# Attention scores as three fp32r matmuls instead of one fp32 matmul, masks added by VectorE

## The chip, the cores and the metric

The program runs on one core of one Trainium2 chip, as one launch. The metric is device time in microseconds (us), the median of several runs. TensorE (PE) multiplies, and its weight loads are a row of their own (PEld). VectorE (DVE), ScalarE (ACT) and GpSimd (POOL) do the elementwise work, and SyncE (SP) issues nearly all DMAs. Each engine takes its instructions in the order in which a scheduler wrote them down when the program was built.

## The reference

Two layers of a mixer with a gated feed-forward net, then retention, another feed-forward net, a short convolution and a mixture of eight experts. All is float32, 256 tokens, width 1024. The change lies in the mixer, which has three branches. Two of them are attentions and one is an mLSTM:

```python
# sparse attention, 8 heads of 64: the 64 best keys of an index score are kept
s = jnp.einsum('bqhd,bqkhd->bhqk', qb, k_sel) * (dh ** -0.5)
s = jnp.where(valid[:, None], s, -jnp.inf); p = jax.nn.softmax(s, axis=-1)
# differential attention, 4 heads x 2 parts of 64, causal
s = jnp.einsum('bqhcd,bshcd->bhcqs', qb, k) * (d ** -0.5)
s = jnp.where(causal, s, -jnp.inf);        p = jax.nn.softmax(s, axis=-1)
a = p[:, :, 0] - lam * p[:, :, 1]
# mLSTM, 4 heads of 128, chunks of 128: a causal mask on the decay matrix
dmat = jnp.where(causal, b_t - b_s + i_s, -jnp.inf)
```

## The kernel before

**Large matmuls.** A weight is loaded as float32 (`raw`, SP's queue, line 210), ScalarE rounds it to fp32r (`hi`, line 222) and VectorE takes the rest (`lo`, line 223). `mm3` (lines 228 to 231) then multiplies hi by hi, hi by lo and lo by hi into one PSUM tile. There are three buffers each of `hi` and `lo`. This work runs through the whole program.

**The mixer.** It runs once per layer, so twice. `ORDER` mixes the chunks of the wide projection with steps of three generators: `dsa` (sparse attention), `diff` (differential attention) and `mlstm`. A scheduler then sets the order on each engine, so that the matmuls of the projection stand between the steps of the attentions.

**Scores.** `qk_rows` normalises and rotates q and k, and `plain_T` (lines 297 to 306) transposes them on TensorE and copies them to SBUF as float32 (`sqT`, `skT`, `dqT`, `dkT`). A head has 64 elements, so its score matmul uses 64 of the 128 rows of the array, the upper or the lower half. Queries come in two tiles `t` of 128, tile 0 against 128 keys and tile 1 against 256. Per layer `dsa` has 8 groups (tile `t`, `q`) of two heads, and `diff` has 8 groups (tile, pair of heads `hp`, part `c`) of two. That is 64 score matmuls over both layers, half of them with 128 keys. After each one a bf16 matmul of the identity `idb` with the mask (`smask` line 607, `negm` line 673) adds 0 or -1e30 into the same PSUM tile. Then VectorE finds the row maximum (`nm`, lines 609 and 675), ScalarE takes the exponential (lines 612 and 678), and TensorE transposes the result (line 543) for the product with v.

**mLSTM.** For each of 4 heads two matmuls with 4 rows (`lf` by `selr`, lines 785 and 787) spread a decay, and after each a bf16 matmul adds `negmT` (lines 786 and 788). ScalarE's exponential (lines 790 and 791) follows.

Of the kernel before, what the change touches and what calls it, by code (L numbers as in the profile page):

```python
# [11 lines left out]
F32R = mybir.dt.float32r  # L12
BF16 = mybir.dt.bfloat16
# [102 lines left out]
class Net:  # L116
# [58 lines left out]

    def masks(self):
        nc, cp = self.nc, self.cp
        self.idb = cp.tile([P, P], BF16, name="idb")
        nc.vector.tensor_copy(self.idb, self.idt)
        self.negm = cp.tile([P, P], BF16, name="negm")  # L180
        nc.vector.tensor_scalar(self.negm, self.lo01, -1.0, BIG, op0=ALU.add, op1=ALU.mult)
        self.negmT = cp.tile([P, P], BF16, name="negmT")
        nc.vector.tensor_scalar(self.negmT, self.up01, -1.0, BIG, op0=ALU.add, op1=ALU.mult)
        self.cap = cp.tile([P, P], F32, name="cap")
        nc.vector.tensor_scalar(self.cap, self.lo01, -0.5, 2.0 * FILL, op0=ALU.add, op1=ALU.mult)
# [238 lines left out]
    def mixer(self, li):  # L424
        nc, tc, I, sp = self.nc, self.tc, self.I, self.sp
        X = self.X
        with ExitStack() as es:
# [5 lines left out]
            def z4(name, shape=(P, 2, 512), dt=F32):  # L433
                return zp_.tile(list(shape), dt, tag="z4", name=name)
# [92 lines left out]
                nc.scalar.activation((skr if c0 == 0 else sv)[:, t], ps, AF.Copy, scale=crs[:, t:t + 1])  # L527
            self.gemm(lambda k: (ch[:, k], cl[:, k]), 2, I["dsa_w_kv_up"][li], [(0, 512), (512, 512)], ev_kv)

            def qk_rows(src, which, dstT):  # L530
                rows = [w2("qkr") for _ in range(2)]
                for t in range(2):
                    normrope(src[:, t], which, rows[t], t)
                self.plain_T(lambda t: rows[t], 4, dstT)

            def pT_of(prow, npair, t):

# [15 lines left out]
            def dsa():  # L553

                smask, scs = [None, None], [None, None]
                for t in range(2):
# [15 lines left out]
                    dsl = slice(t * P, (t + 1) * P)  # L572
                    nc.vector.tensor_tensor(sc[:, dsl], sc[:, dsl], self.cap, op=ALU.min)
                    scs[t] = sc
                sqT, skT = z4("sqT", (P, 4, S)), z4("skT", (P, 4, S))
                qk_rows(zs, 0, sqT)
                yield
                qk_rows(skr, 1, skT)
                yield
                for t in range(2):  # L580
                    nk = P * (t + 1)
# [13 lines left out]
                for t in range(2):  # L595
# [3 lines left out]
                    for q in range(4):  # L599
                        heads = [(q // 2) * 4 + (q % 2) + 2 * j for j in range(2)]  # L600
                        b = slice((q % 2) * 64, (q % 2) * 64 + 64)
                        ps = self.mm_tile()
                        psv = ps.rearrange("p (j s) -> p j s", j=2)[:, :, :nk]
                        for j in range(2):
                            hp = heads[j] // 2
                            nc.tensor.matmul(psv[:, j], sqT[b, hp, t * P:(t + 1) * P], skT[b, hp, :nk], start=True, stop=False)
                            nc.tensor.matmul(psv[:, j], self.idb, smask[t][:, :nk], start=False, stop=True)
                        nm = tp.tile([P, 2], F32, tag="nm", name="nm")
                        nc.vector.tensor_reduce(nm, psv, AX.X, ALU.max, negate=True)
                        pr = w2("pr", (P, 2, 256))  # L610
                        for j in range(2):
                            nc.scalar.activation(pr[:, j, :nk], psv[:, j], AF.Exp, bias=nm[:, j:j + 1],
                                                 accum_out=den[:, heads[j]:heads[j] + 1])
                        pt = pT_of(pr, 2, t)
                        for j, h in enumerate(heads):
                            for s in range(t + 1):
                                nc.tensor.matmul(po[:, h * 64:(h + 1) * 64], pt[:, j, s], sv[:, s, h * 64:(h + 1) * 64],
                                                 start=s == 0, stop=s == t)
                        if q < 3:
                            yield  # L620
# [18 lines left out]
            def diff():  # L639
# [10 lines left out]

                go = tp.tile([P, 1], F32, tag="go", name="go", bufs=1)
                nc.vector.tensor_scalar(go, self.gcol("diff_out_norm_g", li), 1.0 - lam_init, None, op0=ALU.mult)
                dqT, dkT = z4("dqT", (P, 4, S)), z4("dkT", (P, 4, S))
                qk_rows(dq[0], 2, dqT)
                yield
                qk_rows(dk[0], 3, dkT)
                yield
                orow = z4("orow")
                for t in range(2):
                    nk = P * (t + 1)  # L660
                    po = self.mm_tile()
                    for hp in range(2):
# [3 lines left out]
                        for c in range(2):  # L666
# [1 line left out]
                            psv = ps.rearrange("p (j s) -> p j s", j=2)[:, :, :nk]  # L668
                            b = slice(c * 64, c * 64 + 64)
                            for j in range(2):  # L670
                                nc.tensor.matmul(psv[:, j], dqT[b, hp * 2 + j, t * P:(t + 1) * P], dkT[b, hp * 2 + j, :nk],
                                                 start=True, stop=False)
                                nc.tensor.matmul(psv[:, j, t * P:(t + 1) * P], self.idb, self.negm, start=False, stop=True)
                            nm = tp.tile([P, 2], F32, tag="nm", name="nm")
                            nc.vector.tensor_reduce(nm, psv, AX.X, ALU.max, negate=True)
                            pr = w2("dp", (P, 2, 256))
# [97 lines left out]
            def mlstm():  # L774
# [3 lines left out]
                for hp in range(2):  # L778
                    pn = [self.mm_tile() for _ in range(2)]
                    for j in range(2):  # L780
# [1 line left out]

                        pw = self.mm_tile()
                        sel = self.selr[:, h * P:(h + 1) * P]
                        nc.tensor.matmul(pw[:, 0:S], sel, lf[:, 0], start=True, stop=False)
                        nc.tensor.matmul(pw[:, 0:P], self.idb, self.negmT, start=False, stop=True)
                        nc.tensor.matmul(pw[:, S:S + P], sel, lf[:, 0, P:S], start=True, stop=False)
                        nc.tensor.matmul(pw[:, S:S + P], self.idb, self.negmT, start=False, stop=True)
                        wt = w2("wt")[:, 0:384]
                        nc.scalar.activation(wt[:, 0:S], pw[:, 0:S], AF.Exp, bias=ac[:, h:h + 1])  # L790
                        nc.scalar.activation(wt[:, S:], pw[:, S:S + P], AF.Exp, bias=ac[:, 4 + h:5 + h])
# [533 lines left out]
```

## Time and profile before

| | |
|---|---|
| time, 3 runs | 2572.25 to 2575.25 us, median 2572.55 us |
| profiled execution | 2571.89 us, its span 2570.0 us |
| PE busy | 2533.9 us (99%) |
| PEld busy | 2068.1 us (80%) |
| DVE busy | 1888.5 us (73%) |
| ACT busy | 1562.6 us (61%) |
| POOL busy | 65.7 us (3%) |

Matmuls overlap in the pipeline: a row's duration is longer than the time by which it pushes the next one back. What a matmul costs is read as the difference of two starts. The score matmuls start at 94.7 us in layer 0, and the last of layer 1 starts at 704.0 us; the mixer of layer 0 ends near 310 us.

### The profile page before, as it was taken

How to read it: one execution, taken by the hardware profiler on the slowest of the kernel's cores; microseconds unless marked ns; L12 is line 12 of the kernel's file. 1: busy time of each engine (PE TensorE's matmuls, PEld its weight loads, DVE VectorE, ACT ScalarE, POOL GpSimd, SP SyncE). 2: the span in 40 equal slices, each digit the busy share in tenths (PEclk: the TensorE clock that was granted, in tenths of full speed). 3: DMA queues.
4: the chain of work that ended last, by engine and by line, in shares of the span. 5: the costliest groups of instructions: out<-in, count | busy, mean ns of one | idle time of the engine just before them, and what ended most of it. 6: DMA issues, size and time to landing. Idle time of an engine off the chain costs nothing. (4 is left out here: it accounts for less than half of the span.)

```text
span 2570.0 us, 32368 instructions
## 1 busy us (share of the span) xinstructions
PE 2533.9 (99%) x12273; PEld 2068.1 (80%) x12273; DVE 1888.5 (73%) x2427; ACT 1562.6 (61%) x2119; POOL 65.7 (3%) x43
## 2 busy tenths in 40 slices
PE   9999999999999999999999999999999999999998
PEld 8877788878777888778888988888888777877776
DVE  6985755678766556545554778999989898889887
ACT  6555544555555445545444547777777777777776
POOL 1110000020100000000000000000000000000000
PEclk9999999999999999999999999999999999999999
DMA  7443555554445556546555765999999999999993
GB/s 246 149 155 130 166 180 185 160 174 142 148 144 170 190 161 218 164 148 230 195 184 192 268 207 202 347 357 337 360 358 354 330 350 359 344 341 345 365 350 146
DMA packets 324796, 613.75 MB, mean 239 GB/s; under 512 B 10900, under 2 KB 43924, under 8 KB 324504
## 3 DMA queue, kind: packets, MB, share of 16 engines
q1 hardware_dynamic: 324200, 610.98, 69.3%
q8 instruction: 98, 1.61, 0.3%
q10 hardware_dynamic: 432, 0.62, 0.1%
q14 instruction: 66, 0.54, 0.1%
HBM read 610.51 MB, written 1.05 MB: 238 GB/s over the span
## 5 line engine op out<-in xcount | busy, mean ns | idle before, releaser
L223 DVE TENSOR_TENSOR lo<-raw,hi 128x1024 fp32r<-128x1024 f32 (+1 forms) x1156 | 1378.2, 1215 | 569.5 <-ACT hi L222 562.3
L222 ACT CAST hi<-raw 128x1024 fp32r<-128x1024 f32 (+1 forms) x1156 | 1186.5, 1045 | 728.0 <-PE acc L231 367.0
L230 PE MATMUL mm<-lo,gh 128*128 128x512 f32 x896 | 355.4, 397 | 0.3
L229 PE MATMUL mm<-hi,gh 128*128 128x512 f32 x896 | 351.7, 393 | 2.6 <-ACT ST L1131 2.5
L231 PE MATMUL mm<-hi,gl 128*128 128x512 f32 x896 | 351.2, 392 | 0.0
L231 PE MATMUL acc<-hi,hTl 128*128 128x512 f32 x736 | 293.3, 399 | 0.0
L230 PE MATMUL acc<-lo,hTh 128*128 128x512 f32 x736 | 292.2, 397 | 0.0
L229 PE MATMUL acc<-hi,hTh 128*128 128x512 f32 x736 | 292.2, 397 | 0.0
L230 PE MATMUL acc<-lo,xTh 128*128 128x512 f32 (+3 forms) x672 | 252.6, 377 | 2.8 <-DVE lo L223 2.6
L229 PE MATMUL acc<-hi,xTh 128*128 128x512 f32 (+3 forms) x672 | 252.2, 377 | 1.7 <-ACT hi L222 1.6
L231 PE MATMUL acc<-hi,xTl 128*128 128x512 f32 (+3 forms) x672 | 249.8, 374 | 0.0
L229 PE MATMUL mm<-hi,xTh 128*128 128x512 f32 (+1 forms) x608 | 230.5, 379 | 0.0
L231 PE MATMUL mm<-hi,xTl 128*128 128x512 f32 (+1 forms) x608 | 230.0, 378 | 0.0
L230 PE MATMUL mm<-lo,xTh 128*128 128x512 f32 (+1 forms) x608 | 229.8, 378 | 0.0
L230 PEld LDWEIGHTS mm<-lo,gh 128*128 128x128 f32 x896 | 168.3, 188 | 52.3 <-DVE lo L223 15.9
L229 PEld LDWEIGHTS mm<-hi,gh 128*128 128x128 f32 x896 | 168.2, 188 | 40.9 <-ACT ST L1131 3.0
L231 PEld LDWEIGHTS mm<-hi,gl 128*128 128x128 f32 x896 | 168.2, 188 | 36.2
L229 PEld LDWEIGHTS acc<-hi,hTh 128*128 128x128 f32 x736 | 138.5, 188 | 30.6
L230 PEld LDWEIGHTS acc<-lo,hTh 128*128 128x128 f32 x736 | 138.5, 188 | 29.8
L231 PEld LDWEIGHTS acc<-hi,hTl 128*128 128x128 f32 x736 | 138.5, 188 | 29.3
L230 PEld LDWEIGHTS acc<-lo,xTh 128*128 128x128 f32 x672 | 126.3, 188 | 25.0 <-DVE lo L223 4.6
L229 PEld LDWEIGHTS acc<-hi,xTh 128*128 128x128 f32 x672 | 126.1, 188 | 24.2 <-ACT hi L222 2.4
(376 smaller groups left out, 3085.1 us busy)
## 6 DMA issues: line engine op xcount, KB each, us to landing
raw<-in_moe_w_up SPq DMA_DIRECT2D x112, 1024.0 KB, 5.8
raw<-in_moe_w_down SPq DMA_DIRECT2D x112, 1024.0 KB, 5.7
raw<-in_moe_w_gate SPq DMA_DIRECT2D x112, 1024.0 KB, 6.1
raw<-in_w_in SPq DMA_DIRECT2D x52, 1024.0 KB, 5.1
raw<-in_w_gate_up SPq DMA_DIRECT2D x40, 1024.0 KB, 5.0
raw<-in_ret_w_in SPq DMA_DIRECT2D x24, 1024.0 KB, 5.0
raw<-in_w_down SPq DMA_DIRECT2D x20, 1024.0 KB, 5.0
raw<-in_ffn_w_gate SPq DMA_DIRECT2D x14, 1024.0 KB, 5.1
```

Source lines behind the costliest of these rows:

```text
L222: nc.scalar.copy(hi[:, :m], r)
L223: nc.vector.tensor_sub(lo[:, :m], r, hi[:, :m].bitcast(F32))
L229: mm(ps, xh, wh, start=first, stop=False)
L230: mm(ps, xh, wl, start=False, stop=False)
L231: mm(ps, xl, wh, start=False, stop=last)
```

## The change

`qk_rows` now splits the transposed q and k into hi and lo parts (`split_T`: ScalarE rounds, VectorE subtracts) and returns the pair. `scores` calls `mm3`, three fp32r matmuls in place of one fp32 matmul. `add_mask` lets VectorE add the mask to both heads of a group in PSUM. The identity in bf16 and all its matmuls go, those of the mLSTM too. The four tiles of hi and lo parts more in each layer come out of the same ring of 19 buffers (`z4`).

```diff
@@ -175,8 +175,6 @@
 
     def masks(self):
         nc, cp = self.nc, self.cp
-        self.idb = cp.tile([P, P], BF16, name="idb")
-        nc.vector.tensor_copy(self.idb, self.idt)
         self.negm = cp.tile([P, P], BF16, name="negm")
         nc.vector.tensor_scalar(self.negm, self.lo01, -1.0, BIG, op0=ALU.add, op1=ALU.mult)
         self.negmT = cp.tile([P, P], BF16, name="negmT")
@@ -527,11 +525,22 @@
                 nc.scalar.activation((skr if c0 == 0 else sv)[:, t], ps, AF.Copy, scale=crs[:, t:t + 1])
             self.gemm(lambda k: (ch[:, k], cl[:, k]), 2, I["dsa_w_kv_up"][li], [(0, 512), (512, 512)], ev_kv)
 
-            def qk_rows(src, which, dstT):
+            def qk_rows(src, which, name):
+
                 rows = [w2("qkr") for _ in range(2)]
                 for t in range(2):
                     normrope(src[:, t], which, rows[t], t)
-                self.plain_T(lambda t: rows[t], 4, dstT)
+                hl = z4(name + "h", (P, 4, S), F32R), z4(name + "l", (P, 4, S), F32R)
+                self.split_T(lambda t: rows[t], 4, *hl)
+                return hl
+
+            def scores(ps, q, k, b, hp, t, nk):
+
+                ts = slice(t * P, (t + 1) * P)
+                self.mm3(ps, q[0][b, hp, ts], q[1][b, hp, ts], k[0][b, hp, :nk], k[1][b, hp, :nk], True, True)
+
+            def add_mask(v, m, n):
+                nc.vector.tensor_tensor(v, v, m[:, None, :n].to_broadcast([P, 2, n]), op=ALU.add)
 
             def pT_of(prow, npair, t):
 
@@ -572,10 +581,9 @@
                     dsl = slice(t * P, (t + 1) * P)
                     nc.vector.tensor_tensor(sc[:, dsl], sc[:, dsl], self.cap, op=ALU.min)
                     scs[t] = sc
-                sqT, skT = z4("sqT", (P, 4, S)), z4("skT", (P, 4, S))
-                qk_rows(zs, 0, sqT)
+                sqT = qk_rows(zs, 0, "sqT")
                 yield
-                qk_rows(skr, 1, skT)
+                skT = qk_rows(skr, 1, "skT")
                 yield
                 for t in range(2):
                     nk = P * (t + 1)
@@ -602,9 +610,8 @@
                         ps = self.mm_tile()
                         psv = ps.rearrange("p (j s) -> p j s", j=2)[:, :, :nk]
                         for j in range(2):
-                            hp = heads[j] // 2
-                            nc.tensor.matmul(psv[:, j], sqT[b, hp, t * P:(t + 1) * P], skT[b, hp, :nk], start=True, stop=False)
-                            nc.tensor.matmul(psv[:, j], self.idb, smask[t][:, :nk], start=False, stop=True)
+                            scores(psv[:, j], sqT, skT, b, heads[j] // 2, t, nk)
+                        add_mask(psv, smask[t], nk)
                         nm = tp.tile([P, 2], F32, tag="nm", name="nm")
                         nc.vector.tensor_reduce(nm, psv, AX.X, ALU.max, negate=True)
                         pr = w2("pr", (P, 2, 256))
@@ -650,10 +657,9 @@
 
                 go = tp.tile([P, 1], F32, tag="go", name="go", bufs=1)
                 nc.vector.tensor_scalar(go, self.gcol("diff_out_norm_g", li), 1.0 - lam_init, None, op0=ALU.mult)
-                dqT, dkT = z4("dqT", (P, 4, S)), z4("dkT", (P, 4, S))
-                qk_rows(dq[0], 2, dqT)
+                dqT = qk_rows(dq[0], 2, "dqT")
                 yield
-                qk_rows(dk[0], 3, dkT)
+                dkT = qk_rows(dk[0], 3, "dkT")
                 yield
                 orow = z4("orow")
                 for t in range(2):
@@ -668,9 +674,8 @@
                             psv = ps.rearrange("p (j s) -> p j s", j=2)[:, :, :nk]
                             b = slice(c * 64, c * 64 + 64)
                             for j in range(2):
-                                nc.tensor.matmul(psv[:, j], dqT[b, hp * 2 + j, t * P:(t + 1) * P], dkT[b, hp * 2 + j, :nk],
-                                                 start=True, stop=False)
-                                nc.tensor.matmul(psv[:, j, t * P:(t + 1) * P], self.idb, self.negm, start=False, stop=True)
+                                scores(psv[:, j], dqT, dkT, b, hp * 2 + j, t, nk)
+                            add_mask(psv[:, :, t * P:(t + 1) * P], self.negm, P)
                             nm = tp.tile([P, 2], F32, tag="nm", name="nm")
                             nc.vector.tensor_reduce(nm, psv, AX.X, ALU.max, negate=True)
                             pr = w2("dp", (P, 2, 256))
@@ -782,10 +787,9 @@
 
                         pw = self.mm_tile()
                         sel = self.selr[:, h * P:(h + 1) * P]
-                        nc.tensor.matmul(pw[:, 0:S], sel, lf[:, 0], start=True, stop=False)
-                        nc.tensor.matmul(pw[:, 0:P], self.idb, self.negmT, start=False, stop=True)
-                        nc.tensor.matmul(pw[:, S:S + P], sel, lf[:, 0, P:S], start=True, stop=False)
-                        nc.tensor.matmul(pw[:, S:S + P], self.idb, self.negmT, start=False, stop=True)
+                        nc.tensor.matmul(pw[:, 0:S], sel, lf[:, 0], start=True, stop=True)
+                        nc.tensor.matmul(pw[:, S:S + P], sel, lf[:, 0, P:S], start=True, stop=True)
+                        add_mask(pw.rearrange("p (a s) -> p a s", a=2)[:, :, 0:P], self.negmT, P)
                         wt = w2("wt")[:, 0:384]
                         nc.scalar.activation(wt[:, 0:S], pw[:, 0:S], AF.Exp, bias=ac[:, h:h + 1])
                         nc.scalar.activation(wt[:, S:], pw[:, S:S + P], AF.Exp, bias=ac[:, 4 + h:5 + h])
```

TensorE, layer 0, the second pair of heads of `diff` in query tile 0 (four score matmuls; `idb` is the bf16 identity, `negm` the mask). Before:

```order
L693 MATMUL mm<-dv,pT 128x128 x2
L671 MATMUL mm<-dkT,dqT 128x128
L673 LDWEIGHTS idb
L673 MATMUL mm<-negm,idb 128x128
L671 MATMUL mm<-dkT,dqT 128x128
L673 LDWEIGHTS idb
L673 MATMUL mm<-negm,idb 128x128
```

The same place now (`dkTh` and `dqTl` are the hi part of k and the lo part of q):

```order
L698 MATMUL mm<-dv,pT 128x128 x2
L227 MATMUL mm<-dkTh,dqTh 128x128
L228 MATMUL mm<-dkTl,dqTh 128x128
L229 MATMUL mm<-dkTh,dqTl 128x128
L227 MATMUL mm<-dkTh,dqTh 128x128
L228 MATMUL mm<-dkTl,dqTh 128x128
L229 MATMUL mm<-dkTh,dqTl 128x128
```

Before, each head left the 64-row form for a mask of 128 rows. Now twelve matmuls of 64 rows stand in one piece here (six of them shown). Over the program the score matmuls stand in 40 such pieces, where there were 64 of one head each, and 18 of the 64 had another full-height matmul between the head and its mask.

TensorE, layer 0, the first head of `mlstm`. Before:

```order
L785 MATMUL mm<-lf,selr 128x256
L786 LDWEIGHTS idb
L786 MATMUL mm<-negmT,idb 128x128
L787 MATMUL mm<-lf,selr 128x128
L788 LDWEIGHTS idb
L788 MATMUL mm<-negmT,idb 128x128
L793 MATMUL mm<-mqk 128x256
```

And now:

```order
L552 MATMUL mm<-ct,ar 128x128 x4
L790 MATMUL mm<-lf,selr 128x256
L791 MATMUL mm<-lf,selr 128x128
L797 MATMUL mm<-mqk 128x256
L698 MATMUL mm<-dv,pT 128x128 x4
L798 MATMUL mm<-mqk 128x128
```

The two matmuls of the mLSTM's spread now follow each other directly, and the last products of `diff` have moved in behind them.

VectorE, layer 0, from the lo weights ahead of the first pair of heads of `diff` in tile 0 to its end. Before:

```order
L223 TENSOR_TENSOR lo<-raw,hi 128x1024
L844 SCALAR_TENSOR_TENSOR gate<-gate,acc 128x512 x2
L223 TENSOR_TENSOR lo<-raw,hi 128x1024
L675 TENSOR_REDUCE nm<-mm 128x2 x2
L683 RECIPROCAL dden<-dden 128x4
```

And now:

```order
L221 TENSOR_TENSOR lo<-raw,hi 128x1024
L284 TENSOR_TENSOR dkTl<-mm,dkTh 128x512 x2
L221 TENSOR_TENSOR lo<-raw,hi 128x1024
L543 TENSOR_TENSOR mm<-mm,negm 128x2x128 x2
L680 TENSOR_REDUCE nm<-mm 128x2 x2
L688 RECIPROCAL dden<-dden 128x4
```

The subtractions that make the lo part of k and the two mask additions have come into VectorE's queue, between the lo weights, and two gate steps have moved ahead of them.

## Rows read from the trace of the kernel before

**Rows 1.** Page, busy time, share and instructions of each engine.
```profile
PE 2533.9 (99%) x12273; PEld 2068.1 (80%) x12273; DVE 1888.5 (73%) x2427; ACT 1562.6 (61%) x2119; POOL 65.7 (3%) x43
```

**Rows 2.** Stretches of layer 0: us, busy us (x instructions) of each engine.
```profile
60.00:180.00 120.00, 117.65 (x683) 98.12 (x683) 107.99 (x219) 66.72 (x116) 22.19 (x8) 1.00 0.50 157
180.00:310.00 130.00, 128.24 (x619) 99.89 (x617) 83.38 (x133) 69.03 (x157) 4.00 (x4) 1.00 0.44 143
```

**Rows 3.** Timeline of TensorE, 128-key heads: start us, us, instruction.
```profile
179.85 0.39 PE L231 MATMUL acc<-hi,yTl 128*128 128x512 f32 x1
180.08 0.40 PE L229 MATMUL acc<-hi,yTh 128*128 128x512 f32 x1
180.41 0.49 PE L671 MATMUL mm<-dkT,dqT 64*128 64x128 f32 x2
180.99 0.48 PE L671 MATMUL mm<-dkT,dqT 64*128 64x128 f32 x2
```

**Rows 4.** Timeline of the same first head, its passes and second weight load singly.
```profile
180.41 0.37 PE L671 MATMUL mm<-dkT,dqT 64*128 64x128 f32 x1
180.62 0.27 PE L671 MATMUL mm<-dkT,dqT 64*128 64x128 f32 x1
180.51 0.19 PEld L671 LDWEIGHTS mm<-dkT,dqT 64*128 64x128 f32 x1
```

**Rows 5.** Timeline of TensorE, 256-key heads of the two attentions.
```profile
129.32 0.70 PE L606 MATMUL mm<-skT,sqT 64*128 64x256 f32 x2
130.16 0.70 PE L606 MATMUL mm<-skT,sqT 64*128 64x256 f32 x2
...
208.94 0.70 PE L671 MATMUL mm<-dkT,dqT 64*128 64x256 f32 x2
209.73 0.70 PE L671 MATMUL mm<-dkT,dqT 64*128 64x256 f32 x2
```

**Rows 6.** Timeline of TensorE, from 64-row matmuls back to full height.
```profile
54.49 0.39 PE L229 MATMUL acc<-hi,xTh 128*128 128x264 f32 x1
54.72 0.28 PE L230 MATMUL acc<-lo,xTh 128*128 128x264 f32 x1
54.84 0.28 PE L231 MATMUL acc<-hi,xTl 128*128 128x264 f32 x1
```

**Rows 7.** Timeline of TensorE, fp32r matmuls of 256 columns in a row.
```profile
95.45 0.27 PE L263 MATMUL acc<-xTh,lo 128*128 128x256 f32 x1
95.56 0.28 PE L261 MATMUL acc<-xTh,hi 128*128 128x256 f32 x1
```

**Rows 8.** Timeline of TensorE, one head of the mLSTM.
```profile
223.16 0.69 PE L785 MATMUL mm<-lf,selr 4*128 4x256 f32 x2
223.78 0.23 PE L786 MATMUL mm<-negmT,idb 128*128 128x128 bf16 x1
223.94 0.48 PE L787 MATMUL mm<-lf,selr 4*128 4x128 f32 x2
224.42 0.43 PE L793 MATMUL mm<-mqk 128*128 128x256 f32 x1
```

**Rows 9.** Tiles hTh, zp, sqT: count, ns min/median/max, first and last start, forms.
```profile
L285 ACT CAST hTh<-mm x94: 365/587/590, 334.4 to 2546.0; 128x512 fp32r<-128x512 f32 x90, 128x256 fp32r<-128x256 f32 x4
L286 DVE TENSOR_TENSOR hTl<-mm,hTh x94: 413/683/694, 335.6 to 2546.7; 128x512 fp32r<-128x512 f32 x90, 128x256 fp32r<-128x256 f32 x4
L732 DVE TENSOR_TENSOR zp<-acc,bc x16: 411/416/420, 102.6 to 629.1; 128x256 f32<-128x256 f32 x16
L306 ACT COPY sqT<-mm x4: 587/590/595, 73.1 to 565.9; 128x512 f32<-128x512 f32 x4
```

**Rows 10.** Waits to 310 us: us in total, times, longest us.
```profile
PE acc L230 <- DVE lo L223: 1.7, 3, 0.8
PE mm L304 <- DVE qkr L485: 1.5, 1, 1.5
...
DVE nm L675 <- PE mm L673: 8.3, 7, 2.2
```

## Prediction

> **What bounds the kernel now.** I read the page first. TensorE is busy for 99% of the span, VectorE for 73% [rows 1]. So time goes only where TensorE's own work goes, or where TensorE is made to wait. Next come stretches of layer 0. Between 60 and 180 us TensorE is busy for 117.65 of 120 us, but VectorE is close behind with 107.99. From 180 to 310 us VectorE has 46.6 us idle [rows 2]. The reader is to see two engines here: one that is full, and a second that would fill up with 12 us more work. TensorE's waits are few: 1.7 us for lo weights and 1.5 us for the rows of q and k [rows 10].
>
> The rest is read from TensorE's timeline, by differences of starts. A head with 128 keys costs 180.41 to 180.99, 0.58 us with its mask [rows 3]. With 256 keys it costs 0.79 us in `diff` and 0.84 us in `dsa`, whose mask is 256 wide [rows 5].
>
> What is inside the 0.58? An fp32 matmul runs as two passes. The first starts at 180.41 and lasts 0.37, the second at 180.62 and lasts 0.27 [rows 4]. The first is 0.10 longer, since its weights load in the open. The second pass's load starts at 180.51, while the first pass still streams, so it is hidden. That leaves 0.21 - 0.10 = 0.11 us of streaming per pass of 128 columns. The two streams and the open load make 0.32 of the 0.58; the other 0.26 is the mask with the change to 128 rows and back. Coming from a full-height matmul costs too: 180.08 to 180.41 is 0.33 us, where the next head returns from its mask without such a gap [rows 3]; the same matmul costs 0.23 when another follows (179.85 to 180.08), so 0.10 is drain. Going back to full height opens a load again: the first matmul afterwards takes 54.49 to 54.72, 0.23, the next of the same shape 0.12 [rows 6].
>
> **What is removed from TensorE.** 32 heads of 128 keys at 0.58 (18.6), 16 at 0.79 (12.6) and 16 at 0.84 (13.4) make 44.6 us. That is the price of heads in an unbroken piece. The order shows 18 heads with a full-height matmul between score and mask; each such break opens one more load and drain, about 0.2 by the edges above: 3.6 us. Sum 48.2 us.
>
> **What is added on TensorE.** 192 fp32r matmuls of 64 rows. For the 96 with 256 columns the nearest row is the same width at full height, 0.12 us (95.45 to 95.56) [rows 7]. Below lies the pace of loads, 0.10; above lies an fp32 pass of the same shape, about 0.21. I take 0.12, since it is fp32r: 11.5 us. For 128 columns the trace has no fp32r matmul in a stream. Streaming can't be counted at less than the load behind which it stands, 0.10 to 0.11 [rows 4]; above, I take an fp32 pass with twice its streaming, 0.21. I choose 0.107, because 256 columns stream in 0.12: 10.3 us. Both ends stay in the range. To this come 40 stays in the 64-row form, each with drain 0.10, open load 0.10, drain 0.10 and open load 0.11: 0.41 us, 16.4 us in all. Sum 38.2 us, so the scores give back 10.0 us.
>
> **mLSTM.** One head takes 223.16 to 224.42, 1.26 us, until the next matmul, whose load is also open by some 0.06 [rows 8]. Without masks there remain the first pair with its drain (0.62, to 223.78), the second pair's two streams of 0.11, and an open load of 0.11: about 0.95. 8 heads at 0.37 give 3.0 us.
>
> So TensorE loses 13.0 us of work.
>
> **What is added elsewhere.** ScalarE's rounding costs what its copy cost, 587 against 590 ns [rows 9]: nothing. VectorE gets 16 subtractions of 128x512 at 0.68, 8 mask additions of 512 elements at 0.68 and 32 of 256 elements at 0.42 [rows 9] (another row of the same sizes, also reading PSUM): 10.9 + 5.4 + 13.4 = 29.7 us, half in each layer. The 9.8 us of subtractions and `dsa` additions of a layer fall where it had 12 us free, and TensorE's part there gets some 3 us shorter: 107.99 + 9.8 = 117.8 of about 117 us. Something has to slip past 180 us, where room is plenty (46.6 us, of which 5 are taken by the rest). What is queued behind an addition that waits for its scores are lo weights, and TensorE waits for these; before, the row maximum waited in the same place, 8.3 us in total for `diff` in layer 0 [rows 10]. The lower bound is 0, all of it beside TensorE; the upper is 29.7 us, all of it open. I take 3 us, 1.5 per layer, the size of the wait for rows of q and k [rows 10]. The same wait could shrink, as the order now puts eight more projection matmuls ahead of its transposes; I count nothing for that.
>
> The scheduler moved more. The transposes of k in `diff` come later, with projection matmuls put ahead, and the gate biases' loads stand behind weight loads in SP's queue. Four more tiles per layer come from the ring of 19. These are hidden by projection matmuls as long as those last; at the end of layer 0's mixer 75 of them, at 0.23 us, stood between the mLSTM and its transposes in the old order and about 35 in the new. If that cover is gone, a chain of VectorE, ScalarE and GpSimd is late next, and the 3 us grow.
>
> **Sum.** The profiled execution took 2571.89 us, 2570.0 of it span; the median is 0.66 above. 2571.9 - 13.0 + 3.0 = 2561.9 there. As TensorE's gain leaves out smaller edges (a gap of about 0.05 per piece more before than the price of a head holds), I forecast **2561 us**, with a range of its own of 2554 to 2567.
>
> **Rivals.**
> 1. *Narrow fp32r is slow.* If 128 columns of fp32r stream like an fp32 pass, 0.21, the 96 narrow matmuls cost 10.3 us more: 2571 us. For it: no narrow fp32r stream stands in the trace. Against: nothing in the 256-column rows hints at it. Chance 0.20.
> 2. *Weight loads are not hidden in the half array.* Then each of the 192 pays load and stream: 0.21 instead of 0.12 (96 times, 8.6 us) and 0.16 instead of 0.107 (96 times, 5.1 us): 13.7 us more, 2575 us, no gain. Against: the second load started at 180.51, inside the first pass, in the same 64 rows [rows 4]. The Trainium skill, page "TensorE: Matmul & The Clock Gate", section "Part 3: Packing small matmuls — row/col tiling", says that a weight load overlaps running matmuls only when it goes to another row group; by that this rival would hold, and the trace here disagrees, with 0.10 us between the loads. Chance 0.06.
> 3. *VectorE becomes the bound: slower.* In 60 to 180 us it stands at 117.8 of 117 us. If additions and subtractions delay the lo weights behind them instead of slipping, TensorE waits. All 29.7 us open would give 2571.9 - 13 + 29.7 = 2589 us. Slower than before begins when 18 of the 29.7 are open; I put the case at 2579 to 2589. For it: the queue is first in, first out and nearly full. Against: lo weights are done some us ahead through three buffers, and TensorE waited for them only three times. Chance 0.08.
> 4. *Halfway:* 6 to 16 us of VectorE's work come up open, and the change is worth next to nothing: 2565 to 2575 us. Chance 0.08.
>
> **How the numbers follow.** The forecast has 0.58. A measurement of this kernel tells a change from none at about 0.2%, 5.1 us: faster is below 2567.4, slower above 2577.7. Faster: nearly all of the forecast (0.56) and the edges of rivals 1 and 4 (0.06), 0.62. Slower: rival 3 with a piece of rival 2, 0.09. The rest, 0.29, is the same. The range reaches below the forecast's own by 1 us and above to 2576, which takes in rivals 1 and 4, most of 2, and leaves out 3: 2553 to 2576.
>
> **What would show it.** In the changed profile: no `idb` row; groups of six or twelve fp32r score matmuls at 0.11 to 0.12 us from start to start, for 128 and 256 keys alike (rival 1: 0.21 for 128 keys; rival 2: 0.16 and 0.21); a mLSTM head of about 0.95 us; VectorE's busy time 29.7 us up; its stretch from 60 to 180 us at 97% or more; and TensorE's waits for lo weights and for rows of q and k grown by 3 us together. The forecast is wrong if the narrow matmuls are slow, or if waits for VectorE in the two mixers grow by over 8 us.

## The result and the profile after

The changed kernel takes 2599.23 us (median of 5 runs, 2597.98 to 2601.92) against 2573.73 us in the same session: a ratio of 1.0102, interval 1.0088 to 1.0116. It is 25.5 us slower where 12 us faster was forecast. The profiled execution has a span of 2600.0 us, 30.0 more than before.

The page's busy times, to be held against [rows 1]:

```profile
PE 2541.0 (98%) x12257; PEld 2080.7 (80%) x12257; DVE 1912.1 (74%) x2482; ACT 1563.1 (60%) x2119; POOL 68.1 (3%) x43
```

Stretches of the two mixers: us, busy us of PE, PEld, DVE, ACT, POOL, granted clock, DMA share, GB/s ([rows 2] for layer 0).

```profile
60.00:180.00 120.00, 115.75 (x670) 97.12 (x669) 108.31 (x223) 65.05 (x113) 22.22 (x7) 1.00 0.48 154
180.00:310.00 130.00, 119.55 (x558) 96.19 (x557) 85.06 (x143) 62.95 (x143) 6.30 (x6) 0.91 0.38 122
560.00:680.00 120.00, 115.66 (x694) 97.67 (x693) 105.67 (x225) 65.49 (x117) 18.70 (x6) 1.00 0.48 151
680.00:800.00 120.00, 110.67 (x519) 89.21 (x519) 79.94 (x138) 60.87 (x141) 9.82 (x7) 0.91 0.38 128
```

The reader is to see that little happens where VectorE is nearly full (60 to 180 us): TensorE idles there for 4.3 of 120 us where it idled for 2.4. The damage is in the second half of each mixer. In layer 0 TensorE idles for 10.4 of 130 us where it idled for 1.8, with VectorE only two thirds busy, and the granted clock is 0.91 where it was 1.00. TensorE's waits in the changed kernel (us in total, times, longest):

```profile
PE mm L552 <- DVE ar L692: 8.1, 6, 2.9
...
PE mm L801 <- DVE wt L799: 5.9, 2, 3.0
```

The first long one, in its timeline (start us, us, instruction, idle before):

```profile
212.19 0.28 PE L229 MATMUL mm<-dkTh,dqTl 64*128 64x256 f32 x1
...
212.50 0.43 DVE L543 TENSOR_TENSOR mm<-mm,negm 128x256 f32<-128x256 f32 x1 [0.83 <-PE mm L229]
...
217.29 0.39 PE L229 MATMUL acc<-hi,xTl 128*128 128x512 f32 x1
...
217.71 1.04 ACT L220 CAST hi<-raw 128x1024 fp32r<-128x1024 f32 x1 [1.21 <-PE acc L229]
218.66 0.90 ACT L691 ACTIVATE dp<-dp,dden 128x256 f32<-128x256 f32 x2
218.79 1.22 DVE L221 TENSOR_TENSOR lo<-raw,hi 128x1024 fp32r<-128x1024 f32 x1 [1.13 <-ACT hi L220]
219.93 0.87 DVE L692 SCALAR_TENSOR_TENSOR ar<-dp,dden 128x256 f32<-128x256 f32 x2
...
220.56 1.08 PE L552 MATMUL mm<-ct,ar 128*128 128x128 f32 x4 [2.88 <-DVE ar L692]
```

The last score ends at 212.5, and the transposes that need its result start at 220.56: 8 us of mask, maximum, exponentials, scaling and difference, with a hi and a lo of weights ahead of the last two in their queues. In those 8 us the new order gives TensorE 22 projection matmuls, 5 us. The hi even waits for the last of them to free its buffer. TensorE then stands for 2.9 us, and before wt, from 243.0 us on, for 3.0. With each wait the clock falls (the same columns as above):

```profile
217.00:221.00 4.00, 1.12 (x5) 0.64 (x5) 2.64 (x6) 1.85 (x3) 0.00 (x0) 0.85 0.65 189
221.00:230.00 9.00, 7.75 (x30) 6.25 (x30) 3.37 (x6) 3.36 (x9) 0.00 (x0) 0.50 0.19 62
242.00:246.00 4.00, 1.03 (x6) 0.56 (x4) 2.68 (x5) 1.84 (x5) 1.01 (x1) 1.00 0.96 370
246.00:260.00 14.00, 14.00 (x52) 11.66 (x52) 4.49 (x12) 2.96 (x8) 0.00 (x0) 0.54 0.01 2
```

A granted clock of 0.50 is 1.2 of 2.4 GHz. By the trace's clock records it holds from 219.8 (inside the first wait) to 230.0 and from 247.1 (1.2 us behind the second) to 260.8 us, and again for 10.2 us twice in layer 1: 44.4 us. Before, no such stretch stood in the mixers.

**An account of both mixers.** In every trace I took the time from each matmul's start to the next one's, from the start to the first transposes of X, and between the same places of layer 1. What exceeds the median of its kind (the two neighbours' kinds and the form) by more than 0.4 us counts as wait; half of what runs at 1.2 GHz counts as clock; the rest is work, extra matmuls included. In the rows below the first, work, wait, clock and sum are differences from it. It is one execution each, so sums differ from medians; that of e1 was the longest of its four, 2592.53 us. The clock column also holds about 1.7 us, and about 3.4 in e1, e5, e11 and e12, that are not the mixers': between 7 and 15 us the clock stood at 1.2 GHz for 3.4 or 6.8 us in every trace but those of before and e2. "Left" counts the projection matmuls of layer 0 between the first score of `diff` and the transposes of orow in TensorE's order; "heads" those between the spreads of the second and third mLSTM head, alike in both layers.

| kernel | median us | ratio, interval | work | wait | clock | sum | left | heads |
|---|---|---|---|---|---|---|---|---|
| before | 2573.7 | | 575.9 | 14.9 | 0.0 | 590.8 | 212 | 5 |
| changed | 2599.2 | 1.0102 (1.0088-1.0116) | -14.3 | +21.6 | +22.8 | +30.2 | 169 | 3 |
| e1 fp32r, bf16 masks | 2587.1 | 1.0054 (1.0037-1.0071) | +5.3 | +1.1 | +15.0 | +21.4 | 197 | 1 |
| e2 fp32, vector masks | 2583.6 | 1.0043 (1.0027-1.0060) | -14.6 | +15.9 | +10.2 | +11.6 | 183 | 7 |
| e3 first wait filled | 2597.6 | 1.0096 (1.0079-1.0113) | -7.5 | +16.3 | +17.0 | +25.8 | 169 | 3 |
| e4 dsa masks back | 2574.5 | 1.0002 (0.9993-1.0012) | -6.5 | +5.2 | +3.4 | +2.2 | 197 | 8 |
| e5 fp32, diff+mLSTM | 2564.9 | 0.9966 (0.9953-0.9979) | -15.9 | +4.7 | +4.7 | -6.5 | 212 | 8 |
| e6 changed, tap moved | 2569.2 | 0.9989 (0.9979-0.9998) | -13.4 | +8.4 | +1.7 | -3.3 | 194 | 8 |
| e7 diff masks back | 2582.7 | 1.0040 (1.0026-1.0055) | -2.1 | +7.4 | +3.4 | +8.7 | 169 | 8 |
| e8 mLSTM masks back | 2596.2 | 1.0089 (1.0075-1.0104) | -9.4 | +18.1 | +18.1 | +26.9 | 169 | 1 |
| e9 before, tap moved | 2572.8 | 0.9997 (0.9988-1.0006) | -0.9 | +0.3 | +1.7 | +1.2 | 212 | 5 |
| e10 e2, tap moved | 2571.8 | 0.9994 (0.9985-1.0003) | -16.1 | +9.6 | +5.1 | -1.3 | 199 | 8 |
| e11 e5, tap moved | 2564.1 | 0.9961 (0.9948-0.9975) | -16.2 | +4.8 | +4.8 | -6.6 | 212 | 8 |
| e12 fp32, dsa alone | 2595.9 | 1.0085 (1.0069-1.0100) | -3.6 | +8.4 | +21.8 | +26.5 | 183 | 1 |
| e13 e12, heads filled | 2596.2 | 1.0089 (1.0072-1.0106) | +8.2 | +7.1 | +6.8 | +22.1 | 183 | 1 |
| e14 changed, all filled | 2590.1 | 1.0069 (1.0052-1.0085) | +3.4 | +11.9 | +3.4 | +18.7 | 169 | 7 |

### The profile page after: what moved, and what is told of

Same layout as the page of the kernel before. It is cut to its first block, busy times and chain, and to the rows that moved or that the text cites. A ratio compares the mean times of both kernels' runs of the same rounds, so it can differ in the third digit from the quotient of the medians.

```text
span 2600.0 us, 32413 instructions
## 1 busy us (share of the span) xinstructions
PE 2541.0 (98%) x12257; PEld 2080.7 (80%) x12257; DVE 1912.1 (74%) x2482; ACT 1563.1 (60%) x2119; POOL 68.1 (3%) x43
```

## The experiments

The theory to test, "order": the work did shrink, but the scheduler, given longer VectorE chains, set an order in which chains outlast the projection matmuls beside them, and a slow clock follows. The rivals: VectorE's added work itself is the bound; or the fp32r scores are slow.

**e1, all masks as bf16 matmuls again, scores stay fp32r.**

```diff
-                            scores(psv[:, j], sqT, skT, b, heads[j] // 2, t, nk)
-                        add_mask(psv, smask[t], nk)
+                            scores(psv[:, j], sqT, skT, b, heads[j] // 2, t, nk, False)
+                            nc.tensor.matmul(psv[:, j], self.idb, smask[t][:, :nk], start=False, stop=True)
...
-                            add_mask(psv[:, :, t * P:(t + 1) * P], self.negm, P)
...
+                                nc.tensor.matmul(psv[:, j, t * P:(t + 1) * P], self.idb, self.negm, start=False, stop=True)
...
-                        add_mask(pw.rearrange("p (a s) -> p a s", a=2)[:, :, 0:P], self.negmT, P)
...
+                        nc.tensor.matmul(pw[:, 0:P], self.idb, self.negmT, start=False, stop=True)
...
```

> All masks go back to bf16 matmuls; only the scores stay fp32r with hi and lo parts. Order theory (the loss is two waits of TensorE of about 3 us in the second half of each mixer, where the chain from scores to transposes is longer than the projection matmuls placed between, and the 1.2 GHz stretches of 10 to 14 us behind them): this order has 27, 30 and 37 projection matmuls where the changed kernel has 22, 37 and 11, so no long wait and no half clock; TensorE saves about 0.07 us on each of the 32 heads with 256 keys, nothing on those with 128: about 2570 us (2564 to 2577). VectorE theory (its added work comes up open, 23.6 us for 26 us lost): 10.9 of that is left, so about 2580 us. Mask theory (only adding masks on VectorE costs): as the order theory, but with no change of order as its cause.

2587.05 us: all theories missed. The long waits went as the order theory said (+1.1 us). But work rose by 5.3 us instead of falling by 2: between masks, three fp32r matmuls are no cheaper than one fp32 matmul of two passes. Each head's three then stand alone, and the second starts 0.16 us (128 columns) or 0.22 us (256) behind the first, where it is 0.11 and 0.12 inside an unbroken piece. And the clock fell without any wait; TensorE is busy in every microsecond ahead of the fall at 246.5 us:

```profile
242.00:246.00 4.00, 4.00 (x26) 3.17 (x25) 1.54 (x2) 1.60 (x3) 0.00 (x0) 1.00 0.85 289
246.00:250.00 4.00, 4.00 (x19) 3.38 (x19) 0.99 (x4) 0.17 (x2) 0.00 (x0) 0.56 0.27 104
```

What it did in those 4 us is parts of two mLSTM heads (matmuls of 4 rows, of 1 column, of 128 columns) with a single projection matmul between them. Of e1's four other falls in the mixers one, at 751.6 us, stands in the same place of layer 1; the three of 3.4 us stand behind scores with their masks, at 693.6 us after 3.60 of 3.60 us busy.

**e2, scores fp32 again, all masks on VectorE** (`qk_rows` copies q and k again, as before).

```diff
-                self.mm3(ps, q[0][b, hp, ts], q[1][b, hp, ts], k[0][b, hp, :nk], k[1][b, hp, :nk], True, True)
+                nc.tensor.matmul(ps, q[b, hp, ts], k[b, hp, :nk], start=True, stop=True)
```

> The scores go back to single fp32 matmuls with copied operands; only the masks are added by VectorE. Order theory: the order has 24 projection matmuls (5.4 us) before the third group of transposes of ar and only 10 (2.3 us, with 0.9 of mLSTM) before the fourth, against a chain of about 8 us: waits of about 3 and 5 us in each layer with half clock behind them, about 36 us in all, against about 20 us of mask matmuls saved: about 2588 us (2578 to 2600). VectorE theory: 13 to 18 us of added work open against the same saving: 2565 to 2571 us. If fp32r scores are what is slow: 20 us faster than before, about 2553 us.

2583.63 us, inside the order theory's range only. Work is down as in the changed kernel (-14.6), so the whole saving is the masks', none the scores'. So the fp32r scores are out as the cause of the loss. The range held in part by luck: forecast were 36 us of waits and clock against 20 us saved, measured are 26 against 15. Instead of two waits at transposes there was one of 3.0 us per layer, at the scores ahead of the short cover: the next projection matmul needs its PSUM buffer, and the gate step that empties it stands on VectorE behind two additions and two maxima of these scores:

```profile
PE acc L227 <- DVE gate L838: 7.7, 4, 3.0
```

**e3, the first long wait filled.** In `pT_of`, for the first pair of heads of tile 1 of `diff` only:

```diff
+            def keep(ps, dep, n):
+                nc.tensor.matmul(ps[0:2, 0:P], dep, self.ones, start=True, stop=True)
+                for _ in range(n):
+                    nc.tensor.matmul(ps[:, 0:P], self.ones, self.ones, start=True, stop=True)
...
+                if fill is not None:
+                    keep(ps, fill, 9)
...
+                        at = pT_of(ar, 2, t, den[:, 1, 1] if t and not hp else None)
```

> The changed kernel with ten extra matmuls whose results are overwritten (one 2-row product that waits for the denominators, nine 128x128 fp32 of 0.21 us), placed by TensorE in the first long wait of each layer; the order of all other TensorE instructions is the changed kernel's. Order theory with the clock as second part: the wait stays as long, but TensorE is not idle, the stretch at 1.2 GHz from 219.8 to 230.0 us goes away, and some 4 us per layer come back: about 2591 us (2587 to 2595); the second stretch, at 247 us, stays. If the fall of the clock does not hang on the idle TensorE, or costs nothing since VectorE and ScalarE are what is late there: 2599 us or a little above. VectorE theory: 2599 us.

Nothing else moved in TensorE's order, the chain still ends at 220.6 us, and the clock stayed:

```profile
217.00:221.00 4.00, 3.79 (x27) 2.75 (x25) 2.76 (x6) 1.86 (x3) 0.00 (x0) 1.00 0.60 183
220.00:230.00 10.00, 8.41 (x49) 6.67 (x48) 4.81 (x10) 4.95 (x12) 0.00 (x0) 1.00 0.26 99
```

So the idle engine makes the first fall: shown, since filling it is the one difference. In time it won 1.6 us of the 8 expected, so its forecast missed. In the traces the way from the first score of `diff` to the first mLSTM head is 3.3 us shorter in layer 0 and 3.7 in layer 1, nearly the 4 expected; but the second fall of layer 1 grew from 10.2 to 17.1 us, and behind that head layer 1 lost 2.9 us again. That leaves 4.1 us won in the mixers of the profiled execution, more than the medians show.

**e4, dsa masks alone back as bf16 matmuls** (the first four lines of e1).

> The changed kernel with the dsa masks alone back as bf16 matmuls; diff and mLSTM masks stay on VectorE. This puts 9 us back on TensorE (32 heads at 0.26 to 0.3 us) and takes 8 us of VectorE's work away, all of it ahead of the stretch where the time was lost. Order theory: the order has 35, 33 and 15 projection matmuls before the third and fourth transposes of ar and the first use of wt (22, 37 and 11 in the changed kernel), so the first long wait goes, the last shrinks to about 2 us without half clock: about 2570 us (2565 to 2578), although more work was put back on TensorE than was taken off the chains there. VectorE theory: -8 and +9 us: 2600 us.

2574.45 us: 25 us back although TensorE got 8 us of work again. VectorE theory (2600) is out.

**e5, before with the diff and mLSTM masks alone on VectorE.**

```diff
-                                nc.tensor.matmul(psv[:, j, t * P:(t + 1) * P], self.idb, self.negm, start=False, stop=True)
+                            add_mask(psv[:, :, t * P:(t + 1) * P], self.negm, P)
...
-                        nc.tensor.matmul(pw[:, 0:P], self.idb, self.negmT, start=False, stop=True)
-                        nc.tensor.matmul(pw[:, S:S + P], self.idb, self.negmT, start=False, stop=True)
+                        add_mask(pw.rearrange("p (a s) -> p a s", a=2)[:, :, 0:P], self.negmT, P)
```

> The kernel before with the masks of diff and mLSTM alone added by VectorE (24 additions of 256 elements, 10.3 us); scores stay single fp32 matmuls, dsa keeps its bf16 masks. These are the additions that stand in the chains on which TensorE waited. Order theory, as now extended (the number of projection matmuls left behind the first diff score decides whether the chains are covered: 212 before, 169 in the changed kernel, 183 in the run with fp32 scores and all masks on VectorE): here 212 stay, with 27, 31 and 23 ahead of the three chains, so waits grow by only 1 to 3 us per layer and the clock stays at 2.4 GHz; TensorE saves about 5.5 us per layer: about 2566 us (2560 to 2571), faster than before. VectorE theory: 10.3 us of additions open against 11 saved: 2573 us. If an addition in the chain itself is what costs: slower than before, about 2585 us.

2564.85 us, faster than before by 0.34%. The additions in the very chains on which TensorE had waited do no harm while the order covers them:

```profile
180.00:310.00 130.00, 126.09 (x627) 100.95 (x626) 91.13 (x151) 73.44 (x166) 4.34 (x4) 1.00 0.45 150
```

**e6, the changed kernel in full, one convolution tap on ScalarE.**

```diff
-CV = 0
+CV = 1
...
                if CV:
                    nc.scalar.activation(cv, zp[:, 0:S], AF.Identity, scale=tap(0), bias=self.gcol("mlstm_conv_b", li * 8 + j))
```

> The changed kernel in full (fp32r scores, all masks by VectorE), with one of the four taps of mLSTM's convolution computed by ScalarE instead of VectorE (16 operations of 128x256, 0.41 us each, 6.6 us in all, all in the stage ahead of diff). Order theory: 194 projection matmuls stay behind the first diff score (169 without this), with 35, 33 and 15 ahead of the three chains: waits of about 2.5 us per layer more than before in place of 11, at most 3 us of half clock; with some 7 us per layer less TensorE work than before: about 2567 us (2562 to 2574), 32 us less than the changed kernel for 6.6 us of moved work. VectorE theory: 6.6 us less of it: 2593 us. If the clock falls for another reason than the waits and the bunched small matmuls: 2580 us or more.

2569.17 us: 30 us won by moving 6.6 us of VectorE work, with TensorE's own work unchanged within 1 us. The order has 35, 33 and 15 projection matmuls ahead of the chains (22, 37, 11), and neither a wait over 1.5 us nor a fall in the mixers is left:

```profile
180.00:310.00 130.00, 125.21 (x625) 100.15 (x624) 94.36 (x157) 70.92 (x161) 6.81 (x5) 1.00 0.44 146
```

This is not the same each time: two of its twelve runs took 2577.67 and 2579.76 us, with a granted clock of 0.992 and 0.991 over the span where the other ten have 0.994 to 0.997.

**e7 and e8, the changed kernel with the diff masks, or the mLSTM masks, alone back as matmuls** (the lines of e5, reversed).

> The changed kernel with the diff masks alone back as bf16 matmuls (16 additions of 0.43 us off VectorE, out of the chains that waited). Order theory: 169 projection matmuls stay behind the first diff score as in the changed kernel, with 27, 30 and 16 ahead of the three chains; the first long wait of 3 us goes with its 10 us of half clock, the wait before wt and some half clock stay, TensorE gets 3 to 4 us per layer back: about 2588 us (2580 to 2594). VectorE theory: 6.8 us less added work and about 7 us more on TensorE: 2599 us.

> The changed kernel with the mLSTM masks alone back as bf16 matmuls (8 additions of 0.43 us off VectorE). Order theory: the order of TensorE up to the first mLSTM head is that of the changed kernel, so the first wait of 3 us and its half clock stay; before wt there are 17 projection matmuls for 11 and the chain is one addition shorter, so that wait falls to about 1 us and part of the second half-clock stretch goes: about 2590 us (2584 to 2596). VectorE theory: 3.5 us less added work, 3 us more on TensorE: 2599 us.

2582.65 and 2596.17 us; the second is just past the upper edge of its range. In e8 the first wait and its fall stayed, as expected. The second wait did not shrink to 1 us: one of 3.1 us stands in its place in both layers, at a projection matmul whose PSUM buffer a gate step on VectorE has to empty first:

```profile
PE acc L229 <- DVE gate L841: 9.0, 6, 3.1
```

Behind it the clock fell for 13.7 us in layer 0, from 248.5 us on, before the second head began at 251.0. In layer 1 it did not fall, with the same wait, the same order and a single projection matmul between the second and third head. So neither a wait of this size nor such a pair of heads brings a fall each time. e7 shows that "left" does not decide: 169 as in the changed kernel, but 34 us of waits and clock less. What decides is how many of them stand beside each chain: 27, 30 and 16 in e7, 22, 37 and 11 in the changed kernel.

**e9, e10, e11: the tap moved (the edit of e6) in before, in e2 and in e5.**

> Control: the kernel before with the same convolution tap on ScalarE instead of VectorE, nothing else. Order theory: TensorE's order of instructions is the same as before (212 projection matmuls behind the first diff score), it was busy for 99% of the span, so the 6.6 us less on VectorE are worth nothing: 2573 us (2570 to 2575). If the 30 us that the moved tap won in the changed kernel were the tap's own merit: about 2543 us. VectorE theory: 6.6 us less only where VectorE is late, and before it is not: 2573 us as well.

> Scores as single fp32 matmuls, all masks added by VectorE, and the convolution tap on ScalarE. Order theory: 199 projection matmuls stay behind the first diff score (183 without the moved tap), with 27, 30 and 16 ahead of the chains (24, 10 and 20 without): the wait of 3 us before the fourth group goes, about 1 us before wt stays; TensorE has 10 us less mask and score work per layer than before, 2 us of it given back at the edges of transposes; a wait of 2 us in dsa and up to 3 us of half clock per layer stay: about 2565 us (2559 to 2572). VectorE theory: 2584 less 6.6, 2577 us.

> The fp32 scores with the diff and mLSTM masks alone on VectorE, plus the tap on ScalarE. TensorE's order is the same with and without the tap (212 behind the first diff score; 27, 31 and 23 ahead of the chains). Order theory: where the order is the same and the chains are nearly covered, moving 6.6 us off VectorE is worth at most 1 or 2 us: 2564 us (2561 to 2566). VectorE theory: 6.6 us of the 10.3 added are gone: 2558 us.

2572.79, 2571.82 and 2564.08 us. Where TensorE's order stays the same (e9, e11), 6.6 us of VectorE work are worth under 1 us; where the order changes they are worth 12 (e10) or 30 (e6). This settles that VectorE's amount of work is not the price. e10 is at the upper edge of its range.

**e12, before with the dsa masks alone on VectorE.**

```diff
-                            nc.tensor.matmul(psv[:, j], self.idb, smask[t][:, :nk], start=False, stop=True)
+                        add_mask(psv, smask[t], nk)
```

> The counterpart to the run with diff and mLSTM: the kernel before with the dsa masks alone added by VectorE (16 additions, 9 us in all, in the stretch from 60 to 180 us where VectorE was busy for 108 of 120 us); diff and mLSTM keep bf16 masks, scores stay fp32. Order theory: 183 projection matmuls stay behind the first diff score (212 before), so 29 of them, 6.6 us, are used up in the dsa stage; with 27, 30 and 15 ahead of the chains, which have no addition in them, no wait of 3 us comes; but the dsa stage has a wait of its own of about 2 us and half clock of some 3 us per layer as in the run with all masks on VectorE; TensorE saves 4 us per layer: about 2575 us (2570 to 2581), no gain, where the diff and mLSTM additions gained 9 us. VectorE theory: 9 us open against 8 saved: 2574 us (not told apart here by the time, but by where it goes: in the dsa stretch by this theory, behind it by the other).

2595.93 us, 21 above what I expected. The dsa wait has the place and size that I gave it (1.7 us per layer), but 21.8 us went to the clock: 8.5 behind these waits, 10.2 at 246 and 751 us, and the rest at the program's start. At 246 and 751 us again one projection matmul stands between the second and third mLSTM head, but the fall begins ahead of it:

```profile
243.33 0.49 PE L800 MATMUL mm<-mv,wt 128*128 128x128 f32 x2 [0.80 <-DVE wt L798]
...
244.76 0.69 PE L788 MATMUL mm<-lf,selr 4*128 4x256 f32 x2
...
247.07 0.77 PE L230 MATMUL acc<-lo,xTh 128*128 128x512 f32 x1
```

By the clock records it begins at 246.2 us, after a wait of 0.8 us and 2.9 us of one head's products and the next head's spread. In e6 the same wait and nearly the same matmuls passed without a fall. So the second part of my theory was too narrow, as the clock falls here without a long wait; what makes the difference to e6 stays open.

**e13 and e14, extra matmuls ahead of each mLSTM head**, in e12 and, with those of e3, in the changed kernel:

```diff
+            def keep(ps, n):
+                for _ in range(n):
+                    nc.tensor.matmul(ps[:, 0:P], self.ones, self.ones, start=True, stop=True)
...
                         pw = self.mm_tile()
+                        keep(pw, 5)
```

> The kernel with the dsa masks alone on VectorE, with five extra 128x128 fp32 matmuls (0.21 us each, their results are overwritten) ahead of each mLSTM head: 40 of them, 8.5 us of TensorE. If bunched mLSTM heads make the clock fall: no stretch at 1.2 GHz near 246 and 751 us, granted clock of 240 to 260 us at 0.95 or more where it was 0.74; about 10 us come back and 8.5 go, with a wait before wt of 1 us more (9 projection matmuls ahead of it for 15): about 2597 us, no gain in time, but a clock that stays. If the wait before wt makes it fall: the stretches stay, 2604 us or more.

> The changed kernel with the ten extra matmuls in the first long wait and five ahead of each mLSTM head (60 in all, about 13 us, of which 5 lie in waits). The wait of 3 us before wt is not filled. If waits alone make the clock fall: the stretch at 220 us goes, that at 247 us stays: about 2604 us. If bunched heads do, with or without the wait: both go, some 20 us come back for 8 added: about 2588 us, which would leave about 15 us over before less 14 us of saved work as the price of the waits alone.

2596.18 and 2590.05 us, both near what was expected if the heads make the clock fall (e14 by other parts, as its numbers below show). The stretch from 240 to 260 us in e12, in e13 and in e14:

```profile
240.00:260.00 20.00, 19.20 (x86) 14.88 (x85) 6.40 (x14) 6.12 (x20) 1.01 (x1) 0.74 0.23 79
```

```profile
240.00:260.00 20.00, 20.00 (x130) 16.61 (x130) 8.10 (x21) 8.05 (x28) 1.01 (x1) 1.00 0.22 81
```

```profile
240.00:260.00 20.00, 19.75 (x129) 17.25 (x128) 10.31 (x23) 6.77 (x19) 0.00 (x0) 1.00 0.27 90
```

It is not the one profiled execution alone: the granted clock over the span is 0.988 to 0.991 in the four runs of e12 and 0.993 to 0.995 in those of e13, 0.988 to 0.989 in the changed kernel and 0.994 to 0.996 in e14. In e14 work is 17.7 us above the changed kernel's, most of it useless matmuls, and yet the kernel is 9 us faster: the clock gives back 19.4 and the waits 9.7. The fill also shortened the wait before wt (3.0 to 0.3 us, and 0.8 to 0.3 in e13), so these two runs do not tell wait and matmuls apart. In the changed kernel the trace does, in part: the second fall begins at 247.1 us, before the second head's spread at 247.5 (755.7 in layer 1, before the third head), so a small cover between the second and third head can't have begun it. e1 shows that a fall needs no wait.

## Why the prediction was wrong

**The work was sized rightly.** -13.0 us forecast, -14.3 measured. Inside a piece the score matmuls follow each other as forecast, 0.11 us apart with 128 columns and 0.12 with 256; behind the first of a piece, whose load is open, it is mostly 0.16 and 0.22:

```profile
204.18 0.27 PE L227 MATMUL mm<-dkTh,dqTh 64*128 64x128 f32 x1
204.29 0.27 PE L228 MATMUL mm<-dkTl,dqTh 64*128 64x128 f32 x1
...
131.60 0.28 PE L228 MATMUL mm<-skTl,sqTh 64*128 64x256 f32 x1
131.72 0.28 PE L229 MATMUL mm<-skTh,sqTl 64*128 64x256 f32 x1
```

That rejects rivals 1 and 2. The Trainium skill, page "TensorE: Matmul & The Clock Gate", section "Part 3: Packing small matmuls — row/col tiling", says that a weight load overlaps a running matmul only when it goes to another row group. The trace disagrees: the load for the matmul at 131.60 us starts at 131.48, inside the matmul before it (131.37 to 131.76), in the same 64 rows. Rival 1's price was off, too: by [rows 4] an fp32 pass of 128 columns streams in 0.11 us, not 0.21, and 96 x (0.21 - 0.107) is 9.9 us, not 10.3; the forecast does not rest on it. A mLSTM head takes 0.85 us to its next matmul, 0.95 forecast, 1.26 before [rows 8]:

```profile
237.79 0.69 PE L790 MATMUL mm<-lf,selr 4*128 4x256 f32 x2
238.33 0.38 PE L791 MATMUL mm<-lf,selr 4*128 4x128 f32 x2
238.64 0.70 PE L797 MATMUL mm<-mqk 128*128 128x256 f32 x2
```

One thing was hidden in the right sum: it is all the masks'. With the masks on VectorE the fp32r scores change work by 0.3 us (-14.3 against e2's -14.6); with masks between them they cost 5 us (e1).

**VectorE's added work was sized rightly** (30.2 us by the durations of the additions and subtractions, 29.7 forecast; its busy time, in which instructions that overlap count once, rises by 23.6), **but not its stretch.** 60 to 180 us was to fill up to 97%; it stayed at 108.31 of 120. What slipped was `diff`: its first score starts at 193.0 us, 12.6 later than before, and TensorE passed most of that time on 43 projection matmuls that had stood behind it (212 left before, 169 now).

**The step that failed** is the wait: "I take 3 us, 1.5 per layer", with the lost cover of the scheduler's moves ("These are hidden by projection matmuls as long as those last") left without a price of its own. Waits grew by 21.6 us, past the 8 us that I had named as proof against me. The place was wrong as well. I looked for them at lo weights and rows of q and k, which grew by 1.3 us together (lo 2.6 to 3.9, q and k 3.0 in both), and at the end of the mixer, where 35 projection matmuls instead of 75 still covered the chain: the wait there for the transposed result fell from 1.6 to 0.9 us in all. They came earlier, before the transposes of ar (8.1 us) and before wt (5.9), where the steps of the softmax and of the mLSTM stand in the queues of ScalarE and VectorE behind hi and lo of weights. I had counted on the reverse, lo weights behind additions.

**A term was missing:** TensorE's clock, 22.8 us, as much as the waits. The profile before showed 1.00 in both stretches [rows 2], and I took it as given. -14.3 + 21.6 + 22.8 make the 30.2 us by which the profiled executions differ in the mixers; work is what the account leaves over, so the sum closes of itself. Rival 3 had the sign, but neither the size (2579 to 2589 us) nor the mechanism: VectorE was not full where TensorE waited, and its own work was worth under 1 us where the order stayed (e9, e11).

Not settled: why the scheduler picks these orders, which no trace shows. So e6 and e4 show that a small relief of VectorE ahead of `diff` brings the good order back, not that it must. What the changed kernel takes in the order of before was not tried; that the order is the cause is shown by e4, e6, e9 and e11 together, not by that one swap. What decides whether the clock falls, behind small matmuls or a wait, is open too.

The fastest versions here are e5, and e11 with the tap moved: scores in fp32, dsa masks as matmuls, the other masks on VectorE, 2564.85 and 2564.08 us.

## What to carry to other kernels

Where a scheduler sets the order, a changed instruction on a side engine can change the order on the main one (it did in e6, not in e9). Ahead of a prediction, count in the new order what stands beside each chain, and price the chain minus that cover, place by place. Price a new idle stretch of some 3 us twice, once as a wait and once as a possible slow clock behind it: here 3.4 to 17.1 us at half the clock, and once none. Test two parts of a change apart: here one half (masks of `diff` and mLSTM) gains 9 us and the other (dsa masks) alone loses 22.

## What was not expected of the hardware

TensorE's clock fell to 1.2 GHz without an idle engine: in e1 at 246.5 us after 4.00 of 4.00 us busy, and at 693.6 us after 3.60 of 3.60, both times on small matmuls. With one projection matmul between the second and third mLSTM head it fell for 6.8 to 10.2 us in both layers of e1 and e12, and not in layer 1 of e8; in kernels with 5 to 8 there and no fill, for none or 3.4 us. These counts only go together with the falls: in e12 the fall began before that one matmul. In e13 five extra matmuls of 128 x 128 ahead of each head took the falls away, so what stands in that stretch has a part in it; what exactly brings a fall is not shown. The Trainium skill's page "TensorE: Matmul & The Clock Gate", section "Part 1: The HAM clock gate (the "warmup" mystery)", says that the gate goes by how busy the engine has been of late. The busy time of the profile did not show the falls of e1 coming.
